# A hybrid decoder layer: one 128-row buffer and one transposing transfer for the sample's probabilities, two buffers for cache halves, mixing loads three quarters of a tile into the period

## The chip, the cores and the metric

The kernel runs on one core of a Trainium2 chip. The metric is the device time of one execution in microseconds (us). The kernel before took 1815.07 us, the median of three runs (1813.13 to 1816.42).

## The reference, cut to what matters

One layer of a decoder works on a prompt (1024 positions, width 2048) and on a sample (8 sequences of 4 new tokens, each with a cache of 2048 past keys and values for 16 heads of 64). Both pass through the same weights.

```
def _branch_inputs(x, pos, norm_g, w_in, ln_g, ln_b):
    z = _rms_norm(x, norm_g) @ w_in                    # 2048 x 7168
    q, k, v, ga, u, vc, gb = jnp.split(z, SPLITS, axis=-1)
    q, k = _rope(q, pos), _rope(k, pos)
    u = jax.nn.gelu(u)
    vc = _layer_norm(jax.nn.gelu(vc), ln_g, ln_b)
...
# attention: three causal patterns (window, dilation) = (128,1), (512,4), (2048,16),
# merged by their softmax denominators
outs.append(o); lses.append(lse)
return _combine(outs, lses)
...
# mixing, for each chunk of 128 positions and each of 8 groups of 128 channels
mixed = jnp.einsum('gts,bcsgk->bctgk', _masked_spatial(w_s), vr) + jnp.transpose(b_s)[:, :, None]
...
a = o_attn * jax.nn.silu(ga)
c = u * mixed * jax.nn.silu(gb)
return x + jnp.concatenate([a, c], axis=-1) @ w_out    # then a final RMSNorm
```

The kernel computes the three merged patterns as one softmax, whose mask carries for each key the logarithm of the number of patterns that reach it. Of the sample's 2048 past keys 896 are reached, and only those are loaded.

## The kernel before

Every float32 operand of a large product is held as two float16 parts, hi and lo, and a product is three matmuls: hi by hi, hi by lo and lo by hi. `hilo` (L153, L154) makes the parts: ScalarE (ACT) writes hi, VectorE (DVE) writes the rest as lo.

w_in is worked through as 56 tiles of 128 columns and w_out as 16. A weight tile is loaded as float32 in two halves of 1024 columns (`wraw`, L127) and split in four quarters of 512 (`wh` on ACT, L145; `wl` on DVE, L146). `proj_chunk` (L196) multiplies a tile by 352 positions at a time, three times for 1024 prompt and 32 sample positions. After every six of its 48 matmuls (16 slices of the depth by three products) it calls `fill()`, which runs the events whose time has come from a list, `timeline`; times are counted in tiles from the start of a period. The events are attention, cache and mixing steps. The Tile scheduler then settles each engine's queue. Engines work in order; SyncE (SP) issues all the DMAs of this part, in order.

There are eight pairs of heads, and eight periods. `period(p)` multiplies the projection tiles that pair p and the gates need, and beside it runs:

- `prompt_steps(p-1)`, for 8 query tiles x 2 heads, as a pipeline of slots. `fa` makes scores in the bank "s" (L634, L635), DVE's masked minimum `mn` (L643) and ACT's exponential `sp` (L655). `fb` makes the reciprocal `r` (L662) and the probabilities' parts `pn` (L153, L154; three buffers of the tag "pn"), which a transposing transfer turns into `pt` (L671). `fc` multiplies by the values into the one bank "o" (L682, L689); ACT's `ot` (L693) and DVE's `onat` (L694) free it. `gate` transposes `onat` on TensorE (PE) into the bank "t" (L700).
- `sample_steps(p-1)`, for the 8 sequences. `load` fetches the keys, later the values, of one sequence (`kvr`, L735, two buffers). `prep` makes `kvh` (ACT for keys, L743; GpSimd, POOL, for values, L745) and `kvl` (DVE, L746), and asks for the load after next. `s_mm` multiplies with the keys, `soft1` is the softmax over 64 rows (head and token of each sequence) and 928 keys, `soft2` transposes its parts, `pv_mm` multiplies with the values (L842). Both parts of the probabilities lie in buffers of the tag "pn", 64 rows each, and each has a transfer of its own.
- `mix_steps`: `mix_load` (L886 to L897) fetches eight pieces of the normalised vc rows (`vr`), those of the sample (`vrs`), one group's mixing weights (`wr`) and its bias (`bb`). `mix_prep` masks `wr` (L903) and makes its parts `wm`; `mix` multiplies them.

In `period`, `mix_load` is called ahead of the period's first tile, in the periods 1 to 5, 7 and 8, for a group each; one more group is loaded at the start of the last tile of period 8.

Of the kernel before, what the change touches and what calls it, by code (L numbers as in the profile page):

```python
# [9 lines left out]
F16 = mybir.dt.float16  # L10
AF = mybir.ActivationFunctionType
ALU = mybir.AluOpType
# [7 lines left out]
NS = DB * DS  # L20
# [7 lines left out]
NKEY = 896  # L28
NKT = NKEY // 128
# [9 lines left out]
PS = 1024.0  # L39
# [15 lines left out]
def hybrid_step_kernel(  # L55
# [26 lines left out]
    PE, ACT, DVE, POOL, SP = nc.tensor, nc.scalar, nc.vector, nc.gpsimd, nc.sync  # L82
# [69 lines left out]
    def hilo(src, hi, lo, scale):  # L152
        ACT.activation(out=hi, in_=src, func=AF.Copy, scale=scale)  # L153
        DVE.scalar_tensor_tensor(out=lo, in0=src, scalar=scale, in1=hi, op0=ALU.mult, op1=ALU.subtract)  # L154
# [456 lines left out]
    trl = ap_.tile([128, 160], F32, name="trl")  # L611
    SP.dma_start(out=msk, in_=mask_s)
    SP.dma_start(out=trl, in_=tril)

    def wait(c):
        return (c, lambda: None)
# [109 lines left out]
    def sample_steps(p, ahl):  # L726
# [9 lines left out]
            raws[j] = t  # L736

        def prep(j):
            hi = ap_.tile([128, NKEY], F16, tag="kvh", name="kvh", bufs=3)
            lo = ap_.tile([128, NKEY], F16, tag="kvl", name="kvl", bufs=3)  # L740
            r = raws.pop(j)
            if j < DB:
                ACT.activation(out=hi, in_=r, func=AF.Copy, scale=KS)  # L743
            else:
                POOL.tensor_scalar(hi, r, VS, 1.0, ALU.mult, ALU.mult)  # L745
            DVE.scalar_tensor_tensor(  # L746
                out=lo, in0=r, scalar=KS if j < DB else VS, in1=hi, op0=ALU.mult, op1=ALU.subtract
            )
            sts[j] = (hi, lo)
            load(j + 2)  # L750
# [33 lines left out]
        def soft1():  # L784
            stsb = cur["st"]
            ss = ap_.tile([128, S], F32, tag="sp", name="ss", bufs=2)[0:64, 0:NKEY + NS]
            prev = 3e38
            for g in range(2):
                pt = bank(ps_v, "v") if g == 0 else bank(ps_t, "t")
                w = 0  # L790
                for j in range(4):
                    kt = g * 4 + j
                    rows = 128 if kt < NKT else NS
                    PE.transpose(pt[0:64, w:w + rows], stsb[0:rows, kt, :], eye_t[0:rows, 0:rows])
                    w += rows
                mn = ap_.tile([128, 1], F32, tag="mn", name="mn", bufs=4)
                DVE.tensor_tensor_reduce(
                    ss[:, g * 512:g * 512 + w],
                    pt[0:64, 0:w],
                    msk[:, g * 512:g * 512 + w],  # L800
                    1.0 / (QS * KS),
                    prev,
                    ALU.add,
                    ALU.min,
                    mn[0:64],
                )
                prev = mn[0:64]
            den = ap_.tile([128, 1], F32, tag="den", name="den", bufs=6)
            ACT.activation(out=ss, in_=ss, func=AF.Exp, scale=-1.0, bias=prev, accum_out=den[0:64])
            r = ap_.tile([128, 1], F32, tag="r", name="r", bufs=6)  # L810
            DVE.reciprocal(out=r[0:64], in_=den[0:64])
            DVE.tensor_scalar(ss, ss, r[0:64], None, ALU.mult)
            nk = NKEY + NS
            pn = cur["pn"] = [ap_.tile([128, 1024], F16, tag="pn", name="pn", bufs=3) for _ in range(2)]
            for q in pn:
                POOL.memset(q[0:64, nk:1024], 0.0)
            hilo(ss, pn[0][0:64, 0:nk], pn[1][0:64, 0:nk], PS)

        def soft2():
            pst = cur["pst"] = ap_.tile([128, 2, NKT + 1, 64], F16, tag="stp", name="pst", bufs=1)  # L820
            for l, pn in enumerate(cur["pn"]):
                SP.dma_start_transpose(out=pst[:, l], in_=pn[0:64, :])

        def pv_new():
            o = bank(ps_v, "v")
            cur["o"] = o
            v = vsn[p]
            pst = cur["pst"]
            pn = pst[0:NS, :, NKT, :]
            o2 = o[:, 0:128].rearrange("p (l c) -> p l c", l=2)  # L830
            PE.matmul(out=o2, lhsT=v[:, 0, :], rhs=pn, start=True, stop=False)
            PE.matmul(out=o[:, 0:64], lhsT=v[:, 1, :], rhs=pn[:, 0], start=False, stop=False)

        def pv_mm(b):
            o = cur["o"][:, 0:128].rearrange("p (l b c) -> p l b c", l=2, b=DB)
            hi, lo = sts.pop(DB + b)
            pst = cur["pst"]
            for kt in range(NKT):
                c = slice(kt * 128, (kt + 1) * 128)
                pp = pst[:, :, kt, b * 8:(b + 1) * 8]  # L840
                last = b == DB - 1 and kt == NKT - 1
                PE.matmul(out=o[:, :, b, :], lhsT=hi[:, c], rhs=pp, start=False, stop=False)  # L842
                PE.matmul(out=o[:, 0, b, :], lhsT=lo[:, c], rhs=pp[:, 0, :], start=False, stop=last)
# [45 lines left out]
    def mix_load(g):  # L889
        vr = [vr_load(g, 0), vr_load(g, 1)]  # L890
        vrs = ap_.tile([NS, 2, 128], F16, tag="vrs", name="vrs", bufs=1)
        wr = ap_.tile([128, 160], F32, tag="wr", name="wr", bufs=1)
        bb = ap_.tile([128, 160], F32, tag="bb", name="bb", bufs=1)
        gs = slice(g * 128, (g + 1) * 128)
        SP.dma_start(out=vrs, in_=vr_d[NQ, 0:NS, :, gs])
        SP.dma_start(out=wr, in_=wst[g])
        SP.dma_start(out=bb, in_=bst[g].partition_broadcast(128))  # L897
        mixs[g] = (vr, vrs, wr, bb)
# [69 lines left out]
    def period(p):  # L968
        g = p - 1
        pr, ahl = prompt_steps(g)  # L970
        tiles = []
        if g > 0:
            tiles.append((MG[g], ga_evac))
        if p < NP - 1:
            tiles.append((MU[g], u_evac))
        if p < NP - 2:
            tiles.append((MGB[g], gb_evac))
        if p == NP - 1:
            tiles.append((MGB[g - 1], gb_evac))
        if p == NP:  # L980
            tiles += [(MU[g - 1], u_evac), (MGB[g - 1], gb_evac), (MU[g], u_evac), (MGB[g], gb_evac)]
        n = len(tiles)
        if p < NP:
            tiles.append((MV[p], v_evac(p)))
            n = len(tiles) + 2
        end = n - 0.85 if p < NP else n - 0.5
        if g == 0:
            end = n - 0.7
        ev = at(pr, 0.1 if g == 0 else 0.65, end)
        s0 = 0.4 if g == 0 else 0.0  # L990
        ev += [(s0 + t * (n - s0), f) for t, f in sample_steps(g, ahl)]
        mg = None
        if p < NP - 2:
            mg = g
        elif p > NP - 2:
            mg = g - 1
        if mg is not None:
            mix_load(mg)
            if p < NP:
                ready = len(tiles) - 1  # L1000
                pos = (ready - 0.02, ready + 0.12, ready + 0.45, ready + 0.79)
            else:
                pos = (2.95, 3.06, 3.4, 3.72)
            ev += [(t, f) for t, (_, f) in zip(pos, mix_steps(mg))]
        if p < NP:
            ev += at(v_trs(p), end + 0.25, end + 0.5)
        ev.sort(key=lambda e: e[0])
        timeline.extend(ev)
        now[0] = 0.0
        for i, (m, evac) in enumerate(tiles):  # L1010
            w_load(m + 2)
            last = p == NP and i == n - 1
            if last:
                mix_load(g)
            sp = [(i + 0.15 + 0.2 * q, lambda q=q: w_split(m + 1, q)) for q in range(4)]
            if p == NP or i < len(tiles) - 1:
                timeline.extend(sp)
            else:
                timeline.extend([(i + 0.15 + 0.2 * q, lambda q=q: w_split(MA[p], q)) for q in range(4)])
            timeline.sort(key=lambda e: e[0])  # L1020
            for ci, (c0, w) in enumerate(CHUNKS):
                evac(proj_chunk(m, c0, w), c0, w)
                if last:
                    if ci == 2:
                        while timeline:
                            timeline.pop(0)[1]()
                    act_load(slice(0, 7), c0, w)
                    act_load(slice(8, 15), c0, w)
        if p < NP:
            w_load(MB[p] + 1)  # L1030
            for q in range(4):
                w_split(MB[p], q)
            run_ab(p, None)
        assert not timeline
        now[0] = None
        if p == NP:
            for c0, w in CHUNKS:
                act_load(slice(7, 8), c0, w)
# [297 lines left out]
```

## Time and profile before

| | before |
|---|---|
| median of 3 runs | 1815.07 us |
| profiled execution, its own time | 1817.5 us |
| span of that execution, first to last instruction | 1815.7 us |
| granted clock of PE, mean over the span | 0.996 |
| PE busy | 1780.4 us, 98% |
| DVE busy | 1068.4 us, 59% |
| ACT busy | 719.6 us, 40% |
| POOL busy | 118.2 us, 7% |
| bytes read and written by the DMA queues | 276.13 MB |
| main DMA queue, share of 16 engines | 59.6% |

The periods run from about 296 us to 1462 us of the span; what lies before is norms and the first projections, and what lies behind is the product with w_out. In the rows of the profile "L682 MATMUL o<-vst,pt" is the instruction of line 682 that writes o from vst and pt; a number in brackets at the end of a row is the idle time of that engine just before, with what ended it. "SPq" rows are the issue of transfers on SP's queue: the time at which SP sends them and how long that takes. "PEld" is the load of weights into PE, which overlaps its matmuls. In a row of the table by windows stand the stretch, its length, the busy time of PE, PEld, DVE, ACT and POOL with the number of instructions, then the granted clock of PE as a share of full speed, the mean share of the DMA engines that were busy, and what they moved in GB/s.

### The profile page before, as it was taken

Reading aid. Unit: us, or ns where it says so; the run is one execution under the profiler, and the core shown is the slowest. Engines: PE = TensorE matmul, PEld = TensorE weight load, DVE = VectorE, ACT = ScalarE, POOL = GpSimd, SP = SyncE. Lnnn points to the kernel's source line nnn. Section 1 sums busy time; section 2 is a strip of 40 time slices with the busy share of each in tenths; the row PEclk is TensorE's granted clock in tenths of the full one; section 3 lists DMA queues with packets and bytes.
Section 4 is the critical chain, followed back from the end, with each engine's and each line's share of the span. In section 5 each row is a group of like instructions: output and inputs, shape, how many; then the busy total and the mean of one; then the engine's idle time right before and its main releaser. Section 6 shows DMA issues by size and latency. Waiting matters only on the chain. (4 is left out here: it accounts for less than half of the span.)

```text
span 1815.7 us, 37262 instructions
## 1 busy us (share of the span) xinstructions
PE 1780.4 (98%) x15040; PEld 1223.9 (67%) x15040; DVE 1068.4 (59%) x2383; ACT 719.6 (40%) x1605; POOL 118.2 (7%) x139
## 2 busy tenths in 40 slices
PE   8999999999999999999999999999999999999997
PEld 7866666666666666666666666666666666666677
DVE  7733595675666576467557657667656633434343
ACT  7522323542543444354344345345345311312133
POOL 0000020110010010001001000001001100000001
PEclk9999999999999999999999999999999999999999
DMA  7343337677667658567657767767765893333314
GB/s 269 105 101 70 77 117 212 147 182 195 159 141 171 163 130 192 152 157 155 168 156 147 168 184 146 177 189 158 186 179 124 233 340 87 70 77 80 78 46 192
DMA packets 340415, 276.13 MB, mean 152 GB/s; under 512 B 255890, under 2 KB 291730, under 8 KB 338130
## 3 DMA queue, kind: packets, MB, share of 16 engines
q1 hardware_dynamic: 340242, 273.76, 59.6%
q8 instruction: 117, 1.92, 0.4%
q14 instruction: 56, 0.45, 0.1%
HBM read 179.85 MB, written 38.26 MB: 120 GB/s over the span
## 5 line engine op out<-in xcount | busy, mean ns | idle before, releaser
L196 PE MATMUL proj<-xh,wh 128*128 128x352 f16 (+3 forms) x3712 | 1108.0, 303 | 3.4 <-DVE ta L495 1.2
L196 PE MATMUL proj<-xl,wh 128*128 128x352 f16 (+3 forms) x3712 | 1107.6, 303 | 1.6 <-DVE xl L154 1.4
L196 PE MATMUL proj<-xh,wl 128*128 128x352 f16 (+3 forms) x3712 | 1107.4, 303 | 0.0
L196 PEld LDWEIGHTS <-wh 128*128 128x128 f16 x7424 | 697.4, 98 | 323.7 <-issue 3.6
L196 PEld LDWEIGHTS <-wl 128*128 128x128 f16 x3712 | 362.7, 98 | 172.3 <-issue 1.9
L146 DVE SCALAR_TENSOR_TENSOR wl<-wraw,wh 128x512 f16<-128x512 f32 x288 | 193.3, 699 | 136.9 <-ACT wh L145 136.9
L145 ACT ACTIVATE wh<-wraw 128x512 f16<-128x512 f32 x288 | 167.2, 620 | 185.9 <-PE proj L196 180.6
L746 DVE SCALAR_TENSOR_TENSOR kvl<-kvr,kvh 128x896 f16<-128x896 f32 x128 | 141.2, 1103 | 67.2 <-ACT kvh L743 51.5
L655 ACT ACTIVATE sp<-sp,mn 128x256 f32<-128x256 f32 (+7 forms) x128 | 99.0, 773 | 161.1 <-DVE mn L643 159.8
L154 DVE SCALAR_TENSOR_TENSOR pn<-sp,pn 128x512 f16<-128x512 f32 (+2 forms) x192 | 111.7, 591 | 66.3 <-ACT pn L153 65.0
L153 ACT ACTIVATE pn<-sp 128x512 f16<-128x512 f32 (+2 forms) x192 | 96.9, 518 | 44.9 <-DMA pt<-pn 38.0
L745 POOL TENSOR_SCALAR kvh<-kvr 128x896 f16<-128x896 f32 x64 | 63.6, 993 | 778.9 <-DVE r L662 343.0
L743 ACT ACTIVATE kvh<-kvr 128x896 f16<-128x896 f32 x64 | 60.5, 945 | 81.1 <-issue 33.9
L643 DVE CUSTOM_DVE_ANT_0 sp<-s,mp 128x512 f32<-128x512 f32 (+3 forms) x128 | 74.5, 582 | 23.2 <-PE s L635 23.2
L682 PE MATMUL o<-vst,pt 128*128 128x128 f16 x576 | 66.3, 220 | 9.1 <-DVE onat L694 8.7
L154 DVE SCALAR_TENSOR_TENSOR yhl<-proj,yhl 128x352 f16<-128x352 f32 (+1 forms) x42 | 21.4, 509 | 82.0 <-ACT yhl L153 82.0
L153 ACT ACTIVATE yhl<-proj 128x352 f16<-128x352 f32 (+1 forms) x42 | 18.8, 447 | 125.2 <-PE proj L196 96.2
L634 PE MATMUL s<-khd,qst 128*128 128x512 f16 (+2 forms) x192 | 62.8, 327 | 1.9 <-DVE mn L643 1.9
L689 PE MATMUL o<-vst,pt 128*128 128x64 f16 x576 | 62.9, 193 | 0.0
L635 PE MATMUL s<-klo,qst 128*128 128x512 f16 (+2 forms) x192 | 60.2, 327 | 0.0
L689 PEld LDWEIGHTS <-pt 128*128 128x128 f16 x576 | 50.5, 98 | 12.4 <-issue 8.5
L682 PEld LDWEIGHTS <-pt 128*128 128x128 f16 x576 | 52.5, 99 | 6.1 <-DMA pt<-pn 2.3
(191 smaller groups left out, 1486.3 us busy)
## 6 DMA issues: line engine op xcount, KB each, us to landing
wraw<-in_w_in SPq DMA_DIRECT2D x110, 512.0 KB, 4.7
kvr<-in_kc SPq DMA_DIRECT2D x64, 448.0 KB, 3.8
kvr<-in_vc SPq DMA_DIRECT2D x64, 448.0 KB, 3.9
wraw<-in_w_out SPq DMA_DIRECT2D x32, 512.0 KB, 5.0
yn<-in_x SPq DMA_DIRECT2D x8, 1024.0 KB, 13.1
out_y_p<-yn SPq DMA_DIRECT2D x16, 512.0 KB, 3.5
xn<-in_x SPq DMA_DIRECT2D x7, 1024.0 KB, 6.9
out_v_o<-tb SPq DMA_DIRECT2D x24, 176.0 KB, 3.8
```

What stands on the lines that cost most here:

```text
L145: ACT.activation(out=hi[:, sl, :], in_=r[:, rs, :], func=AF.Copy, scale=WS)
L146: DVE.scalar_tensor_tensor(out=lo[:, sl, :], in0=r[:, rs, :], scalar=WS, in1=hi[:, sl, :], op0=ALU.mult, op1=ALU.subtract)
L153: ACT.activation(out=hi, in_=src, func=AF.Copy, scale=scale)
L154: DVE.scalar_tensor_tensor(out=lo, in0=src, scalar=scale, in1=hi, op0=ALU.mult, op1=ALU.subtract)
L196: PE.matmul(out=ps[:, 0:n], lhsT=a[:, k, :], rhs=b[:, k, c0:c0 + n], start=(i == 0), stop=(i == 3 * KT - 1))
L634: PE.matmul(out=ps[:, 0:n], lhsT=qst[h][:, tq], rhs=khd[h][:, j0:j0 + n], start=True, stop=False)
L643: DVE.tensor_tensor_reduce(sp[:, j0:j0 + n], ps[:, 0:n], mp[:, S - nk + j0:S - nk + j0 + n], 1.0 / (QS * KS), prev, ALU.add, ALU.min, mn,)
L655: ACT.activation(out=sp[:, 0:nk], in_=sp[:, 0:nk], func=AF.Exp, scale=-1.0, bias=prev, accum_out=den)
L682: PE.matmul(out=o[:, 0:128].rearrange("p (l c) -> p l c", l=2), lhsT=pt[:, j], rhs=vst[:, :, kb, h * HD:(h + 1) * HD], start=(kb == 0), st ...
L689: PE.matmul(out=o[:, 0:64], lhsT=pt[:, w + j], rhs=vst[:, 0, kb, h * HD:(h + 1) * HD], start=False, stop=(kb == nb - 1))
L745: POOL.tensor_scalar(hi, r, VS, 1.0, ALU.mult, ALU.mult)
L746: DVE.scalar_tensor_tensor(out=lo, in0=r, scalar=KS if j < DB else VS, in1=hi, op0=ALU.mult, op1=ALU.subtract)
```

## The change

There are three edits.

1. The sample's probabilities get a buffer of their own, `spn`, of 128 rows and 1024 columns, whose padding is set to zero once. hi is written to rows 0 to 63 and lo to rows 64 to 127, so that DVE reads rows 0 to 63 and writes rows 64 to 127. One transposing transfer turns both. The layout of `pst` follows: for each key tile the 64 columns of hi, then the 64 of lo. The two buffers of the tag "pn" that the sample took in each period are not asked for any more, and neither are the two settings of padding to zero.
2. `kvh` and `kvl` have two buffers each, not three.
3. `mix_load` of a period is an event at 0.75 of a tile, so it stands in the list between the steps of the sample and the prompt.

```diff
--- before.py
+++ after.py
@@ -611,6 +611,8 @@
     trl = ap_.tile([128, 160], F32, name="trl")
     SP.dma_start(out=msk, in_=mask_s)
     SP.dma_start(out=trl, in_=tril)
+    spn = ap_.tile([128, 1024], F16, name="spn")
+    POOL.memset(spn[:, NKEY + NS:1024], 0.0)
 
     def wait(c):
         return (c, lambda: None)
@@ -736,8 +738,8 @@
             raws[j] = t
 
         def prep(j):
-            hi = ap_.tile([128, NKEY], F16, tag="kvh", name="kvh", bufs=3)
-            lo = ap_.tile([128, NKEY], F16, tag="kvl", name="kvl", bufs=3)
+            hi = ap_.tile([128, NKEY], F16, tag="kvh", name="kvh", bufs=2)
+            lo = ap_.tile([128, NKEY], F16, tag="kvl", name="kvl", bufs=2)
             r = raws.pop(j)
             if j < DB:
                 ACT.activation(out=hi, in_=r, func=AF.Copy, scale=KS)
@@ -811,22 +813,21 @@
             DVE.reciprocal(out=r[0:64], in_=den[0:64])
             DVE.tensor_scalar(ss, ss, r[0:64], None, ALU.mult)
             nk = NKEY + NS
-            pn = cur["pn"] = [ap_.tile([128, 1024], F16, tag="pn", name="pn", bufs=3) for _ in range(2)]
-            for q in pn:
-                POOL.memset(q[0:64, nk:1024], 0.0)
-            hilo(ss, pn[0][0:64, 0:nk], pn[1][0:64, 0:nk], PS)
+            ACT.activation(out=spn[0:64, 0:nk], in_=ss, func=AF.Copy, scale=PS)
+            DVE.scalar_tensor_tensor(
+                out=spn[64:128, 0:nk], in0=ss, scalar=PS, in1=spn[0:64, 0:nk], op0=ALU.mult, op1=ALU.subtract
+            )
 
         def soft2():
-            pst = cur["pst"] = ap_.tile([128, 2, NKT + 1, 64], F16, tag="stp", name="pst", bufs=1)
-            for l, pn in enumerate(cur["pn"]):
-                SP.dma_start_transpose(out=pst[:, l], in_=pn[0:64, :])
+            pst = cur["pst"] = ap_.tile([128, NKT + 1, 2, 64], F16, tag="stp", name="pst", bufs=1)
+            SP.dma_start_transpose(out=pst.rearrange("p k l c -> p k (l c)"), in_=spn)
 
         def pv_new():
             o = bank(ps_v, "v")
             cur["o"] = o
             v = vsn[p]
             pst = cur["pst"]
-            pn = pst[0:NS, :, NKT, :]
+            pn = pst[0:NS, NKT]
             o2 = o[:, 0:128].rearrange("p (l c) -> p l c", l=2)
             PE.matmul(out=o2, lhsT=v[:, 0, :], rhs=pn, start=True, stop=False)
             PE.matmul(out=o[:, 0:64], lhsT=v[:, 1, :], rhs=pn[:, 0], start=False, stop=False)
@@ -837,7 +838,7 @@
             pst = cur["pst"]
             for kt in range(NKT):
                 c = slice(kt * 128, (kt + 1) * 128)
-                pp = pst[:, :, kt, b * 8:(b + 1) * 8]
+                pp = pst[:, kt, :, b * 8:(b + 1) * 8]
                 last = b == DB - 1 and kt == NKT - 1
                 PE.matmul(out=o[:, :, b, :], lhsT=hi[:, c], rhs=pp, start=False, stop=False)
                 PE.matmul(out=o[:, 0, b, :], lhsT=lo[:, c], rhs=pp[:, 0, :], start=False, stop=last)
@@ -995,7 +996,7 @@
         elif p > NP - 2:
             mg = g - 1
         if mg is not None:
-            mix_load(mg)
+            ev.append((0.75, lambda: mix_load(mg)))
             if p < NP:
                 ready = len(tiles) - 1
                 pos = (ready - 0.02, ready + 0.12, ready + 0.45, ready + 0.79)
```

PE's queue is the same, row for row. Those of SP, ACT and DVE differ first at the start of period 1. On SP, before, the mixing loads stand ahead of all else; then come the first weights, the first transposes of the prompt's probabilities, and the cache halves `kvr`:

```order
L886 DMA vr<-vr_d 128x2x128 x8
L895 DMA vrs<-vr_d 32x2x128
L896 DMA wr<-in_wst 128x160
L897 DMA bb<-in_bst 128x160
L127 DMA wraw<-in_w_in 128x1024 x2
L671 DMA_TRANSPOSE pt<-pn 128x2x128
L735 DMA kvr<-in_kc 128x896 x2
L127 DMA wraw<-in_w_in 128x1024
L671 DMA_TRANSPOSE pt<-pn 128x2x128
L896 DMA wr<-in_wst 128x160
L735 DMA kvr<-in_kc 128x896 x2
L671 DMA_TRANSPOSE pt<-pn 128x4x128
```

After, at the same place:

```order
L127 DMA wraw<-in_w_in 128x1024
L737 DMA kvr<-in_kc 128x896 x2
L887 DMA vr<-vr_d 128x2x128 x3
L127 DMA wraw<-in_w_in 128x1024
L737 DMA kvr<-in_kc 128x896
L887 DMA vr<-vr_d 128x2x128 x2
L673 DMA_TRANSPOSE pt<-pn 128x2x128
L887 DMA vr<-vr_d 128x2x128 x3
L896 DMA vrs<-vr_d 32x2x128
L673 DMA_TRANSPOSE pt<-pn 128x2x128
L897 DMA wr<-in_wst 128x160
L898 DMA bb<-in_bst 128x160
```

The two first cache halves moved ahead of the mixing loads, and these stand now between weights, cache halves and transposes; the first `wr` moved from ahead of the first transpose to behind the second. The second `wr` is that of the next group.

On ACT, the same place before. `wh` is a quarter of a weight tile, `ta` belongs to a gate's SiLU or to u's GELU:

```order
L145 ACTIVATE wh<-wraw 128x512 x3
L655 ACTIVATE sp,den<-sp,mn 128x128
L153 ACTIVATE wm<-wr 128x160
L153 ACTIVATE pn<-sp 128x128
L655 ACTIVATE sp,den<-sp,mn 128x128
L153 ACTIVATE pn<-sp 128x128
L208 ACTIVATE ta<-proj 128x352
L743 ACTIVATE kvh<-kvr 128x896
L210 ACTIVATE ta<-tb 128x352
L743 ACTIVATE kvh<-kvr 128x896
L655 ACTIVATE sp,den<-sp,mn 128x256
L153 ACTIVATE pn<-sp 128x256
```

After:

```order
L145 ACTIVATE wh<-wraw 128x512 x2
L745 ACTIVATE kvh<-kvr 128x896
L145 ACTIVATE wh<-wraw 128x512
L745 ACTIVATE kvh<-kvr 128x896
L657 ACTIVATE sp,den<-sp,mn 128x128
L153 ACTIVATE pn<-sp 128x128
L657 ACTIVATE sp,den<-sp,mn 128x128
L153 ACTIVATE pn<-sp 128x128
L208 ACTIVATE ta<-proj 128x352
L210 ACTIVATE ta<-tb 128x352
L657 ACTIVATE sp,den<-sp,mn 128x256
L153 ACTIVATE pn<-sp 128x256
```

The first two casts of cache halves, `kvh`, moved ahead of the first exponential `sp`, and `wm`, the mixing weights' part, moved from behind the first exponential to behind the third item's `pn`.

On DVE, the beginning of the prompt's steps before; "ISA" is the masked minimum:

```order
L643 ISA sp,mn<-s,mp 128x128
L643 ISA mn 128x1
L903 TENSOR_TENSOR wr<-wr,trl 128x160
L662 RECIPROCAL r<-den 128x1
L154 SCALAR_TENSOR_TENSOR wm<-wr,wm 128x160
L154 SCALAR_TENSOR_TENSOR pn<-sp,pn 128x128
L643 ISA sp,mn<-s,mp 128x128
L643 ISA mn 128x1
L662 RECIPROCAL r<-den 128x1
L154 SCALAR_TENSOR_TENSOR pn<-sp,pn 128x128
L209 SCALAR_TENSOR_TENSOR tb<-ta,proj 128x352
L746 SCALAR_TENSOR_TENSOR kvl<-kvr,kvh 128x896
```

After:

```order
L748 SCALAR_TENSOR_TENSOR kvl<-kvr,kvh 128x896
L645 ISA sp,mn<-s,mp 128x128
L645 ISA mn 128x1
L146 SCALAR_TENSOR_TENSOR wl<-wraw,wh 128x512
L664 RECIPROCAL r<-den 128x1
L748 SCALAR_TENSOR_TENSOR kvl<-kvr,kvh 128x896
L154 SCALAR_TENSOR_TENSOR pn<-sp,pn 128x128
L645 ISA sp,mn<-s,mp 128x128
L645 ISA mn 128x1
L664 RECIPROCAL r<-den 128x1
L154 SCALAR_TENSOR_TENSOR pn<-sp,pn 128x128
L209 SCALAR_TENSOR_TENSOR tb<-ta,proj 128x352
```

The first two `kvl` moved into the first item's steps, and `wr` with its `wm` is gone from there. It now stands a few rows on, where before:

```order
L746 SCALAR_TENSOR_TENSOR kvl<-kvr,kvh 128x896
L662 RECIPROCAL r<-den 128x1
L903 TENSOR_TENSOR wr<-wr,trl 128x160
L154 SCALAR_TENSOR_TENSOR pn<-sp,pn 128x256
L643 ISA sp,mn<-s,mp 128x256
L643 ISA mn 128x1
L746 SCALAR_TENSOR_TENSOR kvl<-kvr,kvh 128x896
L694 SCALAR_TENSOR_TENSOR onat<-o,r,ot 128x64
L662 RECIPROCAL r<-den 128x1
```

And after:

```order
L904 TENSOR_TENSOR wr<-wr,trl 128x160
L664 RECIPROCAL r<-den 128x1
L154 SCALAR_TENSOR_TENSOR pn<-sp,pn 128x256
L154 SCALAR_TENSOR_TENSOR wm<-wr,wm 128x160
L645 ISA sp,mn<-s,mp 128x256
L645 ISA mn 128x1
L696 SCALAR_TENSOR_TENSOR onat<-o,r,ot 128x64
L664 RECIPROCAL r<-den 128x1
L904 TENSOR_TENSOR wr<-wr,trl 128x160
L154 SCALAR_TENSOR_TENSOR pn<-sp,pn 128x256
L209 SCALAR_TENSOR_TENSOR tb<-ta,proj 128x352
L212 SCALAR_TENSOR_TENSOR gb<-ta,proj 128x352
```

The first group's `wr` and `wm` moved into the steps ahead of the first `onat`, and the `wr` of the next group moved from ahead of that `onat` to behind it.

## The prediction

> **What bounds the kernel now.** I read the page's first part, then a table by stage, then TensorE's (PE's) own waits between the start of the head-pair periods and their end.
>
> ```profile
> PE 1780.4 (98%) x15040; PEld 1223.9 (67%) x15040; DVE 1068.4 (59%) x2383; ACT 719.6 (40%) x1605; POOL 118.2 (7%) x139
> ```
>
> ```profile
> 295.00:350.00 55.00, 49.25 (x391) 32.19 (x389) 29.07 (x76) 27.00 (x64) 0.93 (x1) 0.94 0.72 179
> 350.00:1462.00 1112.00, 1101.20 (x9716) 749.35 (x9715) 724.56 (x1719) 485.87 (x1080) 90.02 (x103) 1.00 0.70 168
> ```
>
> ```profile
> PE o L682 <- DVE onat L694: 8.7, 4, 5.8
> PE t L700 <- DVE onat L694: 3.7, 4, 1.2
> PE s L634 <- DVE mn L643: 1.9, 3, 0.9
> PE t L700 <- DVE mn L797: 0.7, 1, 0.7
> ```
>
> PE is busy 98% of the span. In the stages that the change can touch it is idle 5.75 us in the first 55 us and 10.8 us in the following 1112. So nothing that takes work off VectorE (DVE), ScalarE (ACT), GpSimd (POOL) or the transfers helps by its own duration; only a PE wait that goes, or one that comes, counts. The longest single wait, 5.8 us, stands at the start of the first period:
>
> ```profile
> 321.07 0.26 PE L682 MATMUL o<-vst,pt 128*128 128x128 f16 x1 [5.75 <-DVE onat L694]
> ```
>
> It costs more than it lasts. In the windows around it the clock column (behind the five busy columns) falls to 0.50:
>
> ```profile
> 315.32:319.74 4.42, 0.00 (x1) 0.10 (x1) 2.62 (x10) 2.01 (x5) 0.00 (x0) 1.00 0.73 182
> 321.07:326.57 5.50, 5.50 (x21) 2.81 (x21) 2.68 (x9) 2.05 (x6) 0.00 (x0) 0.50 0.47 110
> 326.57:330.00 3.43, 3.43 (x28) 2.19 (x27) 0.74 (x4) 0.72 (x3) 0.00 (x0) 1.00 0.33 62
> ```
>
> PE is still at full clock 4.42 us after its last matmul, then drops, and works 5.50 us at half clock, of which 2.75 are lost. The place costs 5.75 + 2.75 = 8.5 us.
>
> Why it waits: PE needs the one bank "o", which DVE's onat frees; that follows ACT's ot, and ot stands in ACT's queue behind a cast kvh that waits for its load.
>
> ```profile
> 313.11 0.95 ACT L743 ACTIVATE kvh<-kvr 128x896 f16<-128x896 f32 x1 [3.78 <-DMA kvr<-in_kc]
> 318.75 0.95 ACT L743 ACTIVATE kvh<-kvr 128x896 f16<-128x896 f32 x1 [1.71 <-DMA kvr<-in_kc]
> 319.61 0.30 ACT L693 ACTIVATE ot<-o,r 128x64 f32<-128x64 f32 x1
> ```
>
> ```profile
> 320.74 0.28 DVE L694 SCALAR_TENSOR_TENSOR onat<-o,r,ot 128x64 f32<-128x64 f32 x1
> ```
>
> And the load is late because SyncE (SP), the only issuer, first sends the mixing loads:
>
> ```profile
> 296.94 5.19 SPq L886 DMA_DIRECT2D vr<-vr_d  x8
> 302.17 0.62 SPq L895 DMA_DIRECT2D vrs<-vr_d  x1
> 302.84 0.58 SPq L896 DMA_DIRECT2D wr<-in_wst  x1
> ...
> 303.94 1.76 SPq L127 DMA_DIRECT2D wraw<-in_w_in  x2
> 307.92 1.23 SPq L671 DMA_TRANSPOSE pt<-pn  x1
> 309.20 1.04 SPq L735 DMA_DIRECT2D kvr<-in_kc  x2
> ...
> 310.82 1.20 SPq L671 DMA_TRANSPOSE pt<-pn  x1
> 312.07 0.58 SPq L896 DMA_DIRECT2D wr<-in_wst  x1
> ```
>
> **The change part by part.** *Mixing loads later.* PE's order is the same row for row. In period 1 SP now sends one wraw, then both kvr, then vr in pieces between the transposes. The first kvr goes out at 296.94 + 0.88 (half the pair 1.76) = 297.8, not 309.2. How long the pieces then take:
>
> ```profile
> kvr<-in_kc SPq DMA_DIRECT2D x2, 448.0 KB, 4.1
> ```
>
> ```profile
> 306.64 0.33 DVE L903 TENSOR_TENSOR wr<-wr,trl 128x160 f32<-128x160 f32 x1 [4.49 <-DMA wr<-in_wst]
> 306.88 0.16 DVE L662 RECIPROCAL r<-den 128x1 f32<-128x1 f32 x1
> 307.37 0.33 DVE L154 SCALAR_TENSOR_TENSOR wm<-wr,wm 128x160 f16<-128x160 f32 x1 [0.33 <-ACT wm L153]
> 307.61 0.28 DVE L154 SCALAR_TENSOR_TENSOR pn<-sp,pn 128x128 f16<-128x128 f32 x1
> 307.81 0.28 DVE L643 CUSTOM_DVE_ANT_0 sp<-s,mp 128x128 f32<-128x128 f32 x1
> ...
> 309.01 0.29 DVE L154 SCALAR_TENSOR_TENSOR pn<-sp,pn 128x128 f16<-128x128 f32 x1 [0.18 <-ACT pn L153]
> ...
> 314.09 1.09 DVE L746 SCALAR_TENSOR_TENSOR kvl<-kvr,kvh 128x896 f16<-128x896 f32 x1 [4.21 <-ACT kvh L743]
> ```
>
> ```profile
> L896 SPq DMA_DIRECT2D wr<-in_wst x8: 372/412/832, 302.8 to 1270.5; - x8
> DMA to landing us min/median/max: 2.6/3.0/4.5
> ```
>
> The first kvr lands at 297.8 + 4.1 = 301.9. Two casts now stand ahead of the first item's exponential on ACT, and their kvl inside DVE's work on it: kvh 0.95, kvl 1.09, then from the minimum to the end of pn 1.5 (307.81 to 309.30), with the second kvl, 1.09, in between. That ends at 306.5, so the first transpose goes out 1.4 us earlier than 307.92. What is late next is wr, the mixing weights. DVE's wr now stands before onat, and wr's load stands behind transpose 1.23, three vr (3/8 of 5.19 = 1.95), vrs 0.62 and transpose 1.20: 306.5 + 5.0 = 311.5. It lands 3.0 later (2.6 to 4.5), at 314.5. From there DVE has wr 0.33, r 0.16, pn and the next minimum, twice as wide as those quoted (about 0.4 each), wm 0.33 and onat 0.28: 2.0 us. PE goes on at 316.6 and not at 321.07: a wait of 1.3, or 2.8 where wr takes 4.5. I take 1.8, since the loads put ahead of it keep the queue full.
>
> A second wr load, for the next group, was issued at 312.07 and now waits for the first wm: SP sends it after the third transpose, which waits for pn at 315.5, so at 316.8, and it lands at 319.8 to 321.3. Behind it DVE has pn, tb, gb and the second onat, some 2.4 us: 322.2 to 323.7. PE wants that one at its next step:
>
> ```profile
> 328.93 0.27 PE L700 MATMUL t<-eye_t,onat 128*128 128x128 f32 x1
> ```
>
> 328.93 - 321.07 = 7.86, less the 2.75 of half clock, is 5.1 after 317.1, so 322.2: a new wait of 0 to 1.5, taken as 0.8. By the Trainium skill's page "DMA: Bandwidth & Descriptors", section "Queues, rings and completion order", each DMA engine takes its descriptors in ring order, which speaks against the change: the small wr would sit behind the kvr and wraw just sent. By that rule the landing would be the 4.5 end, both waits would be at their upper ends (2.8 and 1.5), and the place would gain 4.2 us; the trace's own slowest landing, 4.5 against 3.0, agrees.
>
> The place gains 8.5 - 1.8 - 0.8 = 5.9 us, if no wait is long enough to drop the clock; 4.2 to 7.2 by the ends.
>
> *The sample's own buffer and one transpose.* Sixteen small POOL memsets and eight SP transposes of 1.2 us issue go; both were beside PE's work. The two buffers that the sample took of pn's three are now free for the prompt. Period 4 shows that wait and the PE wait behind it:
>
> ```profile
> 816.70 0.31 ACT L153 ACTIVATE pn<-sp 128x128 f16<-128x128 f32 x1 [1.50 <-DMA pt<-pn]
> ```
>
> ```profile
> 818.51 1.46 DVE L154 SCALAR_TENSOR_TENSOR pn<-ss,pn 64x928 f16<-64x928 f32 x1
> ```
>
> ```profile
> 820.32 0.30 PE L700 MATMUL t<-eye_t,onat 128*128 128x128 f32 x1 [0.68 <-DVE onat L694]
> ```
>
> The PE waits beside this softmax that I can name are this 0.68 and the 0.7 under "mn L797" above, 1.4 in all. The DVE step of 1.46 us stays; its writing to rows 64 to 127 has no row of its own, so its cost is bounded by 0 and by another 1.46 beside PE's work. I count half of the 1.4, 0.7 (0 to 1.4). The new transpose has the shape of the prompt's own.
>
> *Two cache buffers for three.* Each cast is already released by the PE group that frees its buffer; with two, the same cast at the same moment belongs to a group one earlier. What shrinks is the slack:
>
> ```profile
> 548.05 1.08 DVE L746 SCALAR_TENSOR_TENSOR kvl<-kvr,kvh 128x896 f16<-128x896 f32 x1
> ```
>
> ```profile
> 556.03 0.17 PE L842 MATMUL v<-pst,kvh 128*128 128x16 f16 x1
> ```
>
> This one is done at 549.13 and will be wanted at 556.03 instead of a group later: 6.9 us stay, so the edit costs nothing. If DVE came 7 us late there, PE would wait for every further microsecond. In each period one cast moves from POOL to ACT and one back, and a few kvl and pn change places; for that and for what moves in periods 7 and 8 I take 0.3 of new waits (0 to 1.5).
>
> **Sum.** 5.9 + 0.7 - 0.3 = 6.3 us. The profiled execution took 1817.5 (its span is 1815.7), 2.4 above the median shown, so it would be 1811.2 there and 1808.8 against the median.
>
> **The rivals.** *The wait stays long (0.15).* If wr lands near 317.7, 3.2 us later than I sum, PE stands 4.4 us, the clock falls as it does now, and the place still costs 4.4 + 2.75 or more, against 8.5: a gain of at most 1.4 with nothing else, 1813.7. For it speaks that SP's queue is full; against it that the slowest wr took 4.5. Twelve microseconds around another wait of PE, 1.83 long, keep the clock at 1.00:
>
> ```profile
> 1010.00:1022.00 12.00, 10.17 (x98) 6.80 (x94) 10.70 (x22) 6.21 (x14) 1.87 (x2) 1.00 0.78 199
> ```
>
> By the Trainium skill's page "TensorE: Matmul & The Clock Gate", section "Part 1: The HAM clock gate", one idle window of about 3.4 us is enough and the windows run free; by that rule a wait from 3.4 us on could already drop it, so this rival would begin at a landing of 316.7, and the trace's 4.42 us neither confirms nor excludes that.
>
> *Slower: two buffers are too few (0.09).* In the second half of a period DVE's kvl follows a POOL cast among DVE's other work, and the slack is the 6.9 above. If one group in each of the eight periods came 1.5 us too late, that is 12 us: 1808.8 + 12 = 1820.8. It decides against the kernel from 1.3 us on (6.3 + 3.6 over eight). Against it: the order on DVE keeps each kvl at its place.
>
> *Given back elsewhere (0.06).* The first wait shrinks as summed, but the reordered steps of periods 7 and 8 add some 3 us, the size of the waits there now (3.7 and 1.9 in the rows above, with others): 1811.8.
>
> **Chances.** What is left, 0.70, is the forecast, between 1804.5 (8.5 + 1.4 all gained, 1805.2, and 0.7 for the run) and 1811.4. The spread of the runs shown is 3.3 us, so 0.2%, 3.6 us, is about what can be told from no change. Faster by more than that 0.70, within 0.21 (the long wait and the giving back), slower 0.09. The range goes up to 1815.0 to take in both of those and stops short of the slower one.
>
> **What would show it.** PE's longest wait in period 1 below 3 us and the clock at 1.00 through 295 to 350; the first kvr issued before vr; DVE waiting for wr's load at about 312 to 314.5. No ACT wait of pn on a transpose beside the sample's softmax in period 4. No PE wait on kvh or kvl anywhere. I am wrong if the clock still falls in period 1, if PE waits on a cast, or if waits beside onat grow in the steady periods.

## The result and the profile after

The changed kernel takes 1806.69 us, the median of 7 runs (1804.41 to 1810.14); the kernel before takes 1816.42 in the runs beside it (1813.13 to 1819.11). The ratio is 0.995, 95% interval 0.994 to 0.996: 9.7 us faster. 1808.8 was forecast, 6.3 us faster. The time lies in the forecast's range, but two terms of the sum were off by 3 and by 7 us, in opposite directions.

First the page's first part, then the two stages of the table by windows that were shown of before:

```profile
PE 1777.1 (98%) x15040; PEld 1223.6 (68%) x15040; DVE 1069.3 (59%) x2383; ACT 721.2 (40%) x1605; POOL 117.9 (7%) x124
```

```profile
295.00:350.00 55.00, 51.39 (x414) 33.53 (x413) 30.53 (x80) 27.55 (x65) 1.68 (x2) 0.97 0.73 175
350.00:1462.00 1112.00, 1106.25 (x9759) 754.52 (x9757) 727.25 (x1722) 488.31 (x1081) 88.88 (x87) 1.00 0.71 172
```

PE is idle 3.6 us in the first stage (5.75 before) and 5.75 in the second (10.8 before). All of PE's own waits between 295 and 1462 us:

```profile
PE t L702 <- DVE onat L696: 3.6, 6, 1.4
PE o L684 <- DVE onat L696: 2.1, 1, 2.1
PE proj L196 <- DMA xh<-act_d: 2.0, 1, 2.0
PE v L776 <- DVE stsb L765: 0.8, 1, 0.8
PE o L684 <- DMA pt<-pn: 0.6, 1, 0.6
PE s L636 <- DVE mn L645: 0.3, 2, 0.2
```

Before, "o" waited for onat four times and 8.7 us; now once, in period 1. Because PE's order is the same row for row, the starts of its matmuls can be compared one by one. These two rows are the same matmul in period 1, before and then after; the next two the same one behind the periods:

```profile
330.43 0.17 PE L774 MATMUL v<-qbd,kvh 128*128 128x16 f16 x1
```

```profile
327.75 0.17 PE L776 MATMUL v<-qbd,kvh 128*128 128x16 f16 x1 [0.76 <-DVE stsb L765]
```

```profile
1463.89 0.31 PE L196 MATMUL proj<-xh,wh 128*128 128x352 f16 x1 [0.67 <-DMA xh<-act_d]
```

```profile
1453.20 0.31 PE L196 MATMUL proj<-xh,wh 128*128 128x352 f16 x1 [1.95 <-DMA xh<-act_d]
```

The start of period 1 gained 330.43 - 327.75 = 2.7 us, the whole 10.7; so 8.0 came in the steady periods, net of 1.3 that the longer wait for xh at their end takes back.

**Period 1.** The mechanism is the one summed, a little later in each step. The first onat still waits for wr, the second one for the next group's wr:

```profile
297.32 0.90 SPq L737 DMA_DIRECT2D kvr<-in_kc  x2
...
314.28 0.59 SPq L897 DMA_DIRECT2D wr<-in_wst  x1
...
318.47 0.52 SPq L897 DMA_DIRECT2D wr<-in_wst  x1
```

```profile
304.90 0.95 ACT L745 ACTIVATE kvh<-kvr 128x896 f16<-128x896 f32 x1 [4.60 <-DMA kvr<-in_kc]
```

```profile
316.40 0.33 DVE L904 TENSOR_TENSOR wr<-wr,trl 128x160 f32<-128x160 f32 x1 [3.90 <-DMA wr<-in_wst]
...
322.84 0.33 DVE L904 TENSOR_TENSOR wr<-wr,trl 128x160 f32<-128x160 f32 x1 [4.21 <-DMA wr<-in_wst]
```

```profile
318.05 0.22 PE L684 MATMUL o<-vst,pt 128*128 128x128 f16 x1 [2.09 <-DVE onat L696]
```

The wait is 2.09 us, not 5.75. But the clock, which was to stay, falls to 0.50 (the figure behind the five busy columns):

```profile
315.49:318.90 3.41, 1.32 (x11) 0.77 (x9) 1.75 (x8) 1.57 (x6) 0.00 (x0) 1.00 0.75 123
318.90:322.31 3.41, 3.41 (x14) 1.76 (x12) 0.00 (x0) 0.34 (x1) 0.00 (x0) 0.50 0.96 278
```

3.41 us at half clock are 1.7 us lost, beside a wait of 2.1.

**The steady periods.** On ACT, pn of an item beside the sample's softmax in period 2, before and after:

```profile
504.23 0.63 ACT L153 ACTIVATE pn<-sp 128x512 f16<-128x512 f32 x1 [2.18 <-DMA pt<-pn]
```

```profile
498.09 0.63 ACT L153 ACTIVATE pn<-sp 128x512 f16<-128x512 f32 x1
```

The wait for a free pn buffer is gone, and from there the minima, exponentials and onat of this period stand some 2.2 us earlier (mostly 1.6 to 2.4) against PE's rows than before. The next exponential shows it, before and then after, and behind each the same row of PE:

```profile
512.76 0.94 ACT L655 ACTIVATE sp<-sp,mn 128x768 f32<-128x768 f32 x1 [2.24 <-DVE mn L643]
518.10 0.22 PE L913 MATMUL proj<-wm,vr 128*128 128x128 f16 x1
```

```profile
506.41 0.94 ACT L657 ACTIVATE sp<-sp,mn 128x768 f32<-128x768 f32 x1 [2.02 <-DVE mn L645]
513.92 0.22 PE L914 MATMUL proj<-wm,vr 128*128 128x128 f16 x1
```

ACT's row is 6.35 us earlier, PE's 4.18. PE's order is fixed and PE was not waiting for them there, so little shows for some 40 us; then the chain's delay meets PE near the period's end, where 1.3 us are gained in period 2. The largest of those places, in period 5, before and after:

```profile
1016.55 0.22 PE L682 MATMUL o<-vst,pt 128*128 128x128 f16 x1 [1.83 <-DVE onat L694]
```

```profile
1006.62 0.22 PE L684 MATMUL o<-vst,pt 128*128 128x128 f16 x1
```

### The profile page after: what moved, and what is told of

It reads as the page before. It is cut to its first block, busy times and chain, and to the rows that moved or that the text cites. A ratio compares the mean times of both kernels' runs of the same rounds, so it can differ in the third digit from the quotient of the medians.

```text
span 1805.1 us, 37173 instructions
## 1 busy us (share of the span) xinstructions
PE 1777.1 (98%) x15040; PEld 1223.6 (68%) x15040; DVE 1069.3 (59%) x2383; ACT 721.2 (40%) x1605; POOL 117.9 (7%) x124
## 3 DMA queue, kind: packets, MB, share of 16 engines
q8 instruction: 117, 1.92, 0.4%
## 5 line engine op out<-in xcount | busy, mean ns | idle before, releaser
L684 PEld LDWEIGHTS <-pt 128*128 128x128 f16 x576 | 52.4, 98 | 4.8 <-issue 0.9
L695 ACT ACTIVATE ot<-o,r 128x64 f32<-128x64 f32 x128 | 39.0, 304 | 41.5 <-PE o L691 41.1
```

What stands on the lines that cost most here:

```text
L684: PE.matmul(out=o[:, 0:128].rearrange("p (l c) -> p l c", l=2), lhsT=pt[:, j], rhs=vst[:, :, kb, h * HD:(h + 1) * HD], start=(kb == 0), st ...
```

## The experiments

Theory B is the sum of the prediction. Theory A was formed from the two traces: the own buffer carries most of the gain. Theory C came after the first four runs. All kernels were timed beside the kernel before; PE's order is that of before in each of them. Ratios are to the kernel before, with 95% intervals; rows are of one profiled execution of each kernel.

| kernel | median, us | before, us | ratio |
|---|---|---|---|
| changed kernel | 1806.69 | 1816.42 | 0.995 [0.994, 0.996] |
| mix_only | 1812.60 | 1816.26 | 0.9976 [0.9968, 0.9985] |
| kv_only | 1815.66 | 1815.95 | 0.9995 [0.9984, 1.0005] |
| spn_only | 1805.45 | 1815.95 | 0.9943 [0.993, 0.9955] |
| mix_undone | 1802.73 | 1816.26 | 0.993 [0.9917, 0.9943] |
| two_transfers | 1805.14 | 1816.26 | 0.9942 [0.9929, 0.9955] |
| pn4 | 1799.70 | 1816.26 | 0.9907 [0.9892, 0.9923] |
| pn4_mix | 1803.04 | 1815.95 | 0.9928 [0.9915, 0.994] |
| pn4_p1 | 1805.09 | 1815.95 | 0.9939 [0.9925, 0.9952] |
| pn4_kvr_first | 1798.51 | 1816.73 | 0.9907 [0.9891, 0.9924] |
| after_again | 1807.20 | 1816.73 | 0.9954 [0.9937, 0.997] |
| mix78_undone | 1807.26 | 1816.73 | 0.9955 [0.9938, 0.9972] |
| kvh_undone | 1804.32 | 1816.73 | 0.9942 [0.9927, 0.9957] |

**mix_only: the mixing loads moved, nothing else.**

```diff
 if mg is not None:
-    mix_load(mg)
+    ev.append((0.75, lambda: mix_load(mg)))
```

> The kernel before, with the mixing loads moved to 0.75 of a tile and nothing else. Theory A, from the comparison of the two traces (PE's rows one by one): the move is worth about 2.7 us at the start of period 1, since the wait there fell from 5.75 to 2.1 us but the clock still dropped for 3.4 us; so 2 to 4 us faster than before in all. Theory B, the sum of the prediction: the move carries nearly the whole change, 5.9 us or more, so 6 to 9 us faster. In both, PE's wait for the first onat of period 1 is near 2 us; A says that the waits for onat near the ends of the periods 2 to 5 stay as before.

3.7 us faster. PE's first wait in period 1 is 2.48 us, put down to a transpose, and the clock stays at 1.00:

```profile
317.93 0.23 PE L682 MATMUL o<-vst,pt 128*128 128x128 f16 x1 [2.48 <-DMA pt<-pn]
```

Between 350 and 1445 us PE waits 7.8 us in all, against 10.1 before. Theory A's number holds, though not by the clock drop that A took it from: without one, this execution is 3.9 us ahead once PE is past the start of period 1. The 6 to 9 us of B do not hold.

**mix_undone: the other two edits, the loads back at the start.**

```diff
-            ev.append((0.75, lambda: mix_load(mg)))
+            mix_load(mg)
```

> The changed kernel with the mixing loads back at the start of the period: the sample's own buffer with one transfer, and two cache buffers. Theory A: the own buffer lets the prompt's steps run 1.4 to 2.4 us ahead from the sample's softmax to the period's end, and the wait for onat behind it goes in each period; 6 to 8 us faster than before, with the 5.75 us wait in period 1 back as it was. Theory B: 0 to 1.5 us faster (0.7 less 0.3 in the sum).

13.5 us faster than before, and faster than the whole change: A named the right part, but neither theory had this. The wait in period 1 did not come back:

```profile
318.11 0.22 PE L684 MATMUL o<-vst,pt 128*128 128x128 f16 x1 [2.16 <-DVE onat L696]
```

ACT's queue tells why. With two buffers the third cast of a cache half has no free one, so ot, which frees PE's bank, stands right behind pn and not behind that cast, as at 318.75 before:

```profile
316.55 0.42 ACT L153 ACTIVATE pn<-sp 128x256 f16<-128x256 f32 x1
316.87 0.30 ACT L695 ACTIVATE ot<-o,r 128x64 f32<-128x64 f32 x1
```

So two edits take away the same wait by different routes. This became theory C.

**pn4: buffers or transfers?** Two cache buffers and four of the tag "pn"; the sample still takes two of them, with two transfers.

```diff
-hi = ap_.tile([128, NKEY], F16, tag="kvh", name="kvh", bufs=3)
+hi = ap_.tile([128, NKEY], F16, tag="kvh", name="kvh", bufs=2)
...
-pn = ap_.tile([128, 1024], F16, tag="pn", name="pn", bufs=3)
+pn = ap_.tile([128, 1024], F16, tag="pn", name="pn", bufs=4)
```

(and the same for kvl, and for the sample's pn)

> The kernel before with two cache buffers for three and, from the room that this frees, four buffers of the tag pn instead of three; the sample's probabilities still take two of them and two transfers, and the mixing loads stay at the start. It tells whether buffers or transfers make the lead. If buffers (A1): with two left for the prompt in place of one, most of the lead is there, 4 to 8 us faster than before. If the transfer saved on SP (A2): no change, within 1 us. By B: within 1 us.

16.6 us faster, more than either theory gave. All of PE's waits between 295 and 1462 us are then:

```profile
PE proj L196 <- DMA xh<-act_d: 2.5, 1, 2.5
PE o L682 <- DVE onat L694: 2.3, 1, 2.3
PE o L682 <- DMA pt<-pn: 0.3, 1, 0.3
```

The page's group for pn on ACT has the reason in its last figure, the idle time before it that ended with a transpose. Before, after, and pn4:

```profile
L153 ACT ACTIVATE pn<-sp 128x512 f16<-128x512 f32 (+2 forms) x192 | 96.9, 518 | 44.9 <-DMA pt<-pn 38.0
```

```profile
L153 ACT ACTIVATE pn<-sp 128x512 f16<-128x512 f32 (+2 forms) x192 | 96.7, 518 | 31.8 <-DMA pt<-pn 29.0
```

```profile
L153 ACT ACTIVATE pn<-sp 128x512 f16<-128x512 f32 (+2 forms) x192 | 94.7, 516 | 12.8 <-DMA pt<-pn 9.2
```

Four shared buffers help at two places. Beside the sample's softmax of period 2 the first pn still waits 1.92 us (2.18 before), but the second one no longer does (0.63 before): onat runs 0.6 to 0.8 us ahead there and 1.4 to 2.0 later in the period, and PE gains the same 1.3 us over that period as in the changed kernel. And they help with the last items of a period, whose second pn waits even in the changed kernel (here near the end of period 5):

```profile
998.61 0.63 ACT L153 ACTIVATE pn<-sp 128x512 f16<-128x512 f32 x1 [2.90 <-DMA pt<-pn]
```

**two_transfers: the own buffer, but each half turned by itself.**

```diff
-SP.dma_start_transpose(out=pst.rearrange("p k l c -> p k (l c)"), in_=spn)
+for l in range(2):
+    SP.dma_start_transpose(out=pst[:, l], in_=spn[64 * l:64 * l + 64])
```

> The changed kernel with the own buffer of 128 rows kept, but its halves turned by two transfers of 64 rows as before, and the old order of pst; everything else as changed. A1 (buffers): as fast as the changed kernel within 1 us, some 9 us faster than before. A2 (one transfer): the lead is gone, 3 us faster than before. B says nothing of it beyond 0 to 1 us slower than the changed kernel.

11.1 us faster than before: no slower than the changed kernel, with an interval that overlaps it. The saved transfer is worth nothing that shows; the lead is the buffers' (A1).

**kv_only: two cache buffers, nothing else.** The edit is the one shown at pn4, without pn.

> The kernel before with two cache buffers for three and nothing else. Theory C, formed after the first runs: with two buffers the third cast kvh of period 1 can no longer stand ahead of ot on ACT, so PE's wait for the first onat falls from 5.75 to about 2.2 us without the mixing loads being moved; 3.5 us faster than before, and up to 6 where the clock does not drop. The waits at the ends of the periods 2 to 5 stay. By the prediction's pricing (the edit costs nothing): no change, within 1 us.

No change that can be told: 0.9995. Its profiled execution shows the gain of theory C and where it goes. The first wait fell to

```profile
316.86 0.22 PE L682 MATMUL o<-vst,pt 128*128 128x128 f16 x1 [2.28 <-DVE onat L694]
```

and by the same comparison of PE's rows that execution was 6.9 us ahead of before at 320 us of its span (the clock did not drop there), but only 4.6 behind the periods. The prompt is still short of pn buffers (ACT's pn waits 38.1 us for transposes, 38.0 before), and PE's waits for onat at "t" between 350 and 1445 us are 5.4 us, against 3.7 before; with all others there they are 10.7, against 10.1:

```profile
PE t L700 <- DVE onat L694: 5.4, 4, 2.4
```

The 11 runs lie between 1810.37 and 1819.37. The profiled one (1812.92) is 2.7 us faster than their median, and that of before (1817.5) 1.5 slower than the median beside it, so most of the 4.6 is the choice of these two executions; why a gain of 3 us or more in period 1 does not show in the medians is open. In period 2 PE gains nothing here, nor in mix_only (they fall back 0.3 and 0.1 us between 480 and 630 us of before), while every kernel with the own buffer or the fourth pn gains 0.6 to 1.3 there.

**spn_only: the own buffer with one transfer.** Loads at the start, three buffers of kvh (two of kvl, since the room does not hold three).

> The changed kernel with the mixing loads back at the start and three buffers of kvh again (kvl keeps two, since the room does not hold three). Theory C: the wait of 5.75 us in period 1 and its clock drop are back as in the kernel before, and the own buffer alone gives the lead behind the sample's softmax; 7 to 10 us faster than before, 3 to 6 us slower than with two buffers of kvh. If the lead were the work of the two cache buffers instead: within 2 us of the kernel before.

10.5 us faster than before. PE's first wait in period 1 is long again, with a clock drop (3.4 us at half clock; 6.8 before):

```profile
319.78 0.26 PE L684 MATMUL o<-vst,pt 128*128 128x128 f16 x1 [4.41 <-DVE onat L696]
```

and the waits between 350 and 1445 us are down from 10.1 us to 2.6. The lead is the own buffer's. With two buffers of kvh the median is 2.7 us lower (1805.45 to 1802.73), but the runs are from two chips and the intervals overlap; PE's rows put 2.1 of it at the start of period 1.

**pn4_mix: does the move still help?** pn4 with the edit of mix_only.

> Two cache buffers, four buffers of the tag pn that prompt and sample share (two transfers for the sample), and the mixing loads moved as in the change. Theory C: beside two cache buffers the move has nothing left to win at the first onat and costs 1.3 us at the next steps of period 1 and about 2 us in period 7: 3 to 5 us slower than the same kernel without the move, 11 to 13 us faster than before. Theory B': the move gains its 3 to 4 us here too, 19 to 20 us faster than before.

12.9 us faster than before, 3.3 us slower than pn4 by the medians, as C gave; the two were timed on different chips, and their intervals overlap. The rows of PE put 3.2 us of cost at the start of period 1: t waits for onat for 2.0 us there, and the sample's first product for stsb for 0.8.

**pn4_p1: an attempt that missed.** In period 1 alone wr goes out ahead of all, the rest at 0.75 of a tile.

```diff
+            wr_load(mg)
+            if p == 1:
+                ev.append((0.75, lambda: mix_load(mg)))
+            else:
+                mix_load(mg)
```

> A version that should beat both: two cache buffers, four buffers of the tag pn, mixing loads at the start of every period but the first, where all but the mixing weights wr come at 0.75 of a tile and wr ahead of all else. The first onat then waits for neither the third kvh nor wr: its wait of 2.2 us goes. Theory C: 1 to 4 us faster than the same kernel with all mixing loads at the start (pn4, 16.6 us faster than before), so 17 to 20 us faster than before. If something else is late next there, 14 to 17.

10.9 us faster: slower than even the second case gave. The first wait went as meant (0.48), but the wr of the next group, which DVE takes before the second onat, came later still, and the clock dropped:

```profile
324.86 0.33 DVE L910 TENSOR_TENSOR wr<-wr,trl 128x160 f32<-128x160 f32 x1 [7.96 <-DMA wr<-in_wst]
```

```profile
327.29 0.48 PE L700 MATMUL t<-eye_t,onat 128*128 128x128 f32 x1 [4.71 <-DVE onat L694]
```

**pn4_kvr_first: cache halves first, mixing loads right behind them.**

```diff
+        ss_ev = sample_steps(g, ahl)
+        if p == 1:
+            ss_ev.pop(0)[1]()
+            ss_ev.pop(0)[1]()
```

The two steps called at once are the loads of the first two halves.

> Two cache buffers, four buffers of the tag pn shared by prompt and sample, and in period 1 the first two cache halves asked for ahead of the mixing loads, which keep their place at the start of every period. The first casts then have their data before the first exponential, and the weights wr of the mixing still come in time: PE's wait of 2.3 us for the first onat of period 1 goes, and none comes at the second one. Theory C: 1 to 4 us faster than the same kernel with the mixing loads first (0.9907 of before), so 18 to 21 us faster than before. If wr is late again, as in the version with the loads at 0.75 of a tile: 11 to 15.

18.2 us faster than before and 8.7 faster than the changed kernel timed beside it (1807.20); its ratio is that of pn4. All of PE's waits from 295 to 1462 us:

```profile
PE proj L196 <- DMA xh<-act_d: 1.3, 1, 1.3
PE v L774 <- DVE stsb L763: 0.8, 1, 0.8
PE t L700 <- DVE onat L694: 0.5, 1, 0.5
PE o L682 <- DVE onat L694: 0.2, 1, 0.2
```

The 2.3 us at the first onat are gone as expected; 1.6 come back at the steps behind it, the second onat among them, where no wait was expected. The 1 to 4 us over pn4 do not show: what is won is less than the intervals.

**after_again, mix78_undone, kvh_undone: what of the change costs, and where.** The changed kernel again; then with

```diff
-            ev.append((0.75, lambda: mix_load(mg)))
+            if p < 7:
+                ev.append((0.75, lambda: mix_load(mg)))
+            else:
+                mix_load(mg)
```

and then with three buffers of kvh.

> The changed kernel once more, on the same chip as the others of this call, so that the versions with a part undone are compared with it directly. 8 to 10 us faster than before, as measured.

> The changed kernel with the mixing loads of the periods 7 and 8 alone back at the start of the period. Theory C, from the rows of PE: of the 4 us that the move costs beside the other two edits, 1.3 arise in period 1 and 2.4 in period 7; so 2 to 3 us faster than the changed kernel. If the cost in period 7 is a matter of chance between executions: no difference, within 1 us.

> The changed kernel with three buffers of kvh again, mixing loads at 0.75 of a tile. Theory C: the two edits take away the same wait in period 1, so that with the loads moved the third buffer costs nothing; within 1.5 us of the changed kernel. If the two edits add up: 2 to 3 us slower than the changed kernel.

after_again confirms the first timing. mix78_undone is the changed kernel's equal (1807.26): theory C's place for the cost was wrong. The wait in question stands at the end of period 6, and it is there with the loads of the periods 7 and 8 at the start, too:

```profile
1146.89 0.33 PE L702 MATMUL t<-eye_t,onat 128*128 128x128 f32 x1 [1.25 <-DVE onat L696]
```

kvh_undone has a median 2.9 us lower than after_again, with overlapping intervals, which is outside both expected cases: beside the move, the third kvh buffer costs nothing, as C said, and whether it helps is not settled.

## Why the prediction was right, and where it was not

The time came out near the sum by luck as much as by its mechanism. Of the 6.3 us, 5.9 were to come from period 1 and 0.7 from the buffer; PE's rows give 2.7 and 8.0, and the two errors cancel for the most part. One of the prediction's own signs of being wrong came, the clock's fall in period 1. The others did not: no wait on a cast, and PE's waits for onat did not grow in the steady periods taken together (3.4 us between 350 and 1445 us, 6.6 before). Beside the softmax of period 4 pn's wait of 1.50 us has shrunk to 0.40, and one of 1.99 just ahead of it is gone.

- **Mixing loads, first wait.** Summed: wr issued at 311.5, landed at 314.5, a wait of 1.3 to 2.8. Measured: issued at 314.28, taken up by 316.40, a wait of 2.09. The first cast began at 304.9, not at 301.9, because its load took over 7 us, not 4.1, with vr and weights in flight beside it; wr was issued 2.8 us late by that, landed faster (2.0 us, not 3.0), and PE itself came 0.6 later. The second wait, taken as 0.8, is 1.1 (0.36 more than usual at t, 0.76 at stsb). By the Trainium skill's page "DMA: Bandwidth & Descriptors", section "Queues, rings and completion order", each DMA engine consumes its descriptors in ring order; the prediction took from it that both small loads would land late, behind those ahead. The second did, DVE taking it up 4.4 us after its issue began; the first did not, at 2.1.
- **The step that failed there: the clock.** The place was to gain 5.9 "if no wait is long enough to drop the clock"; it gained 2.7. A 2.09 us wait dropped it, though the 1.83 at 1016 us before had not; the 2.48 of mix_only and the 2.31 of pn4 did not either, so the length of the wait does not decide (the last section has what does). The rival "the wait stays long" had the drop begin at 3.4 or 4.4 us.
- **The own buffer, priced at 0.7, was the main gain.** This is the term that was sized wrong: 0.7 in the sum, 8.0 in the rows. The sum had the row with ACT's wait (816.70, 1.50 us) and counted only PE waits beside it. The delay is carried by the chain to the period's end, where it is charged to onat. spn_only gives 10.5 us for the edit by itself (with kvl at two buffers); its profiled execution is 12.2 us ahead in all, 2.4 of that at the start of period 1.
- **Two cache buffers, priced at nothing.** By themselves they measure so. Beside the own buffer PE's rows give them 2.1 us at the start of period 1, by a route that the sum did not look at: the cast that can't be placed any more. The medians neither contradict nor settle it. The cast it watched, in the steady periods, never made PE wait; the rival "two buffers are too few" did not come.
- **The terms do not add.** Singly the edits give 3.7 + 0.3 + 10.5 = 14.5 us, together 9.7. Moving the loads gains 3.7 us where the third cast is still in the way, and costs 3 to 4 us by the medians where it is not (1802.73 against 1806.69; 1799.70 against 1803.04): both pairs have one sign, and in each the intervals just overlap.
- **One transfer for two, and rows 64 to 127.** DVE's step with the shifted rows takes 1.12 us in four periods and 1.35 in the other four, the old one 1.12 and 1.46; two_transfers shows no cost of the second transfer.

What stays open: why the changed kernel's pn waits 1.92 us at the end of period 6 (1.21 in after_again) for a transpose that SP issues at the same place, where mix_undone's waits 0.38; the loads of the periods 7 and 8 are not the cause.

## What to carry to other kernels

Where two pipelines draw from one set of buffers, look for the second one's late buffer in the first one's queue, and follow the delay down its chain to the next place where the bounding engine is due: the price stands there, under another instruction's name, and not beside the wait. Edits that remove the same wait do not add, so time each of them alone and left out. A transfer moved out of one load's way is in another's way next.

## What the runs showed of the hardware that was not expected

In these traces the clock falls by idle time within one period of a fixed grid, not by the length of a wait. Every drop and return of the clock between 280 and 1480 us lies a whole number of 3.413 us after the first rise (before: 89 to the drop, 2 more to the return; the drop behind the last matmuls comes 434 after that). Counting PE's idle time in each such window (its matmuls' ends are modelled), the clock dropped behind windows with 1.98, 2.05, 2.09, 2.16, 2.24, 2.27, 2.52 and 3.41 us idle, and behind none with 1.80 or less, in 14 traces. In before the window right after the drop, with 1.33 us idle at half clock, was followed by another at half clock. Four such windows, of two_transfers and spn_only (the clock fell right behind them) and of mix78_undone and pn4_mix (it did not):

```profile
314.18:317.59 3.41, 1.43 (x12) 0.84 (x10) 1.59 (x7) 1.08 (x4) 0.00 (x0) 1.00 0.49 83
```

```profile
1415.28:1418.69 3.41, 1.36 (x22) 1.09 (x21) 3.30 (x10) 1.56 (x7) 0.00 (x0) 1.00 0.37 57
```

```profile
314.54:317.95 3.41, 1.61 (x11) 0.94 (x10) 1.31 (x7) 0.54 (x2) 0.00 (x0) 1.00 0.51 70
```

```profile
323.73:327.14 3.41, 1.72 (x13) 1.11 (x14) 1.68 (x7) 1.97 (x7) 0.00 (x0) 1.00 0.20 38
```

So a wait of 2 to 2.3 us costs 1.7 more when it falls into one window, as the 2.09 in the changed kernel, and nothing more when the grid cuts it in two, as the 2.31 in pn4 (1.26 and 1.05). The grid's place differs from execution to execution (the first rise lies between 13.5 and 16.5 us in these traces), so by this the same kernel's time can move by the 1.7 us of one drop (an estimate; no kernel was profiled both with and without its drop). The Trainium skill's page "TensorE: Matmul & The Clock Gate", section "Part 1: The HAM clock gate", has windows of this length that run free, with which the traces agree, and asks for an idle one; there the measurement decides: 1.98 of 3.41 us idle, 58%, was enough, and 1.80, 53%, was not.
